# First half's attention: softmax weights moved by a transfer, then transposed as fp32r

## The chip, the cores and the metric

The kernel runs on one core of one Trainium2 chip. The metric is the device time of one execution in microseconds; of the kernel before there are three such runs. One further execution was recorded by the hardware profiler, and everything said of engines, waits and transfers comes from it. The five engines are TensorE (PE; its weight loads are shown apart as PEld), VectorE (DVE), ScalarE (ACT), GpSimd (POOL) and SyncE (SP). SP does no arithmetic here, its queue only issues transfers; POOL's queue issues most of the others.

## The reference, cut to what matters

The program is a two-layer network over 1024 latent tokens and 256 context tokens with 1024 features. Layer 0 mixes tokens with a convolution module, layer 1 with grouped-query attention; each is followed by a SwiGLU feed-forward block. The change lies in the attention of layer 1, for the latent tokens (16 query heads, 4 key/value heads, 64 features a head, 1024 + 256 = 1280 keys):

```python
def gqa_sdpa(q, k, v):
    B, Q, H, Dh = q.shape
    qg = q.reshape(B, Q, N_KV_HEADS, KV_GROUP, Dh)
    s = jnp.einsum("bqkgd,bskd->bkgqs", qg, k).astype(jnp.float32) * (Dh ** -0.5)
    p = jax.nn.softmax(s, axis=-1).astype(v.dtype)
    o = jnp.einsum("bkgqs,bskd->bqkgd", p, v)
    return o.reshape(B, Q, H * Dh)
```

Everything is fp32 in the reference.

## The kernel before, in words

**Arithmetic.** Products of fp32 matrices are made from fp32r operands: a value is split into a high part, rounded to fp32r, and a low part, the rest (`split`, lines 161 and 164; weights in `wload`, lines 144 and 148), and three products are added up (`mm3`, lines 172 to 174).

**The attention's unit.** One unit is one key/value head `t` and 128 queries `qt`: four query heads against 1280 keys. The first half of the queries has 16 units, the second half another 16. A unit has two generators. `scores` (line 1116) multiplies queries and keys for one head at a time into a region of 1280 columns of PSUM; VectorE scales the result into SBUF and finds its minimum (line 1122), ScalarE takes the exponential in place and sums it (line 1124). The place is one of the slots of the list `pring`. `values` goes over ten blocks of 128 keys: four transposes, one for each head, into one bank of PSUM (line 1134, with the constant identity as the moving operand and the softmax weights as the stationary one); a copy to fp32r on ScalarE (line 1137); the low part on VectorE (line 1138); two matmuls with the values' high and low halves, each 512 columns wide (lines 1140 and 1141). At the end the two halves are added and divided by the sums (lines 1145 to 1156), and the result is stored to DRAM (line 1450).

**How they are interleaved.** `attn_stream` goes through the units. After each head's scores of a unit it advances the previous unit's `values` by some blocks, as the tuple `turns` says: 3, 3, 3 and 2 of its eleven steps when at least four slots are free. The program's order is the priority of each instruction; a planner then sets each engine's order before the kernel runs, with its own costs, and takes whatever is ready in its plan with the highest priority. At run time each engine works strictly in that order. `later` (the value matmuls, with `lav` = 40) gives a lower priority.

**The stages around it.** While the first units run, the last three of the four query projections of the right half are pumped in beside them from the background queue `bgq`, at `rate` 0.8. They read the normalised tokens in the tiles T4 and T6 and use T5 for work. When the queue is empty, `attention` takes T5 for three more slots (ten in all), and the score region in PSUM gets a second place (`sring`). After the last unit of the first half, the second half's units start in the background beside the output projection of the first half (`out_proj`), which loads the attention's result into HS, splits it into T6 and T3, and writes T4; the feed-forward block follows. The second half's slots lie in T1 and T5.

**Queues.** In this stage POOL's queue carries the loads of queries (line 1102) and keys (line 1095) and the stores of results (line 1450). SP's queue carries the projection's weights (line 143).

Of the kernel before, what the change touches and what calls it, by code (L numbers as in the profile page):

```python
# [8 lines left out]
F32 = mybir.dt.float32  # L9
F32R = mybir.dt.float32r  # L10
# [5 lines left out]
P = 128  # L16
# [4 lines left out]
TOK = CTX + SEQ  # L21
# [19 lines left out]
NC_, NL = CTX // PH, SEQ // PH  # L41
# [14 lines left out]
class Kern:  # L56
# [51 lines left out]
    def acc(self, n):  # L108
        return self.sp.tile([P, 512], F32, tag="acc", name="acc", bufs=2)[:, :n]

    def tiny(self, shape, name):
        return self.sp.tile(shape, F32, tag=name, name=name, bufs=2)

    @contextmanager
    def later(self, n=32):
# [464 lines left out]
    def shift(self):  # L580

        nc, cv = self.nc, self.cvs["C"]
        self.part = self.tiny([P, NC_], "part")
        nc.vector.tensor_scalar(out=self.part, in0=self.vsum[:, :NC_], scalar1=KT / (KT - 1.0), scalar2=None,
                                op0=ALU.mult)
        self.about = self.by_token(self.part)
        self.cacc = self.acc(CTX)
        for k in range(KT - 1):
            self.centre(k)
            yield  # L590
# [514 lines left out]
    def scores(self, q, rq, kt, slots, Ps, sums):  # L1105

        nc = self.nc
        for h in range(4):
            o = self.sring[self.si % len(self.sring)]
            self.si += 1  # L1110
            sc = self.ps.rearrange("p b n -> p (b n)")[:, o:o + TOK]
            k0 = 0
            while k0 < TOK:
                w = min(512 - (o + k0) % 512, TOK - k0)
                for p in range(2):
                    nc.tensor.matmul(sc[:, k0:k0 + w], lhsT=q[:, h, :], rhs=kt[:, p * TOK + k0:p * TOK + k0 + w],  # L1116
                                     start=p == 0, stop=p == 1)
# [4 lines left out]
            nc.vector.tensor_scalar(out=pt, in0=sc, scalar1=rq[:, h:h + 1], scalar2=None, op0=ALU.mult, op1=ALU.min,  # L1122
                                    accum_out=mn)
            nc.scalar.activation(pt, pt, AF.Exp, bias=mn, scale=-1.0, accum_out=sums[:, 0, h:h + 1])
            Ps.append(pt)
            yield 1.07

    def values(self, t, Ps, sums, dst, done):
        nc, c = self.nc, self.c
        av = self.bank("av")  # L1130
        for j in range(NJ):
            tp = self.bank("pt")
            for h in range(4):
                nc.tensor.transpose(tp[:, h * P:(h + 1) * P], Ps[h][:, j * P:(j + 1) * P], c["ident"])  # L1134
            ph, pl = self.ptring[self.ptslot % len(self.ptring)]
            self.ptslot += 1
            nc.scalar.copy(ph, tp)  # L1137
            nc.vector.tensor_tensor(pl, tp, ph.bitcast(F32), op=ALU.subtract)  # L1138
            with self.later(self.lav):
                nc.tensor.matmul(av, lhsT=self.value(t, j), rhs=ph, start=j == 0, stop=False)  # L1140
                nc.tensor.matmul(av, lhsT=self.value(t, j), rhs=pl, start=False, stop=j == NJ - 1)  # L1141
            yield 0.87
# [16 lines left out]

    def attn_stream(self, units, kts, dst_of, loaded=False):  # L1160

        prev, cur, nq, Ps = None, None, None, []
        for n, (t, qt) in enumerate(units):
            if t != cur:
                if cur is not None and len(kts) == 1 or cur is None and not loaded:
                    self.load_k(t, kts[t % len(kts)])
                cur, kt = t, kts[t % len(kts)]
            q = nq or self.load_q(t, qt)
            nq = self.load_q(*units[n + 1]) if n + 1 < len(units) else None
# [9 lines left out]
            sg = self.scores(q, self.rq[t][:, 4 * qt:4 * qt + 4], kt, slots, Ps, sums)  # L1179
# [250 lines left out]
    def attention(self, final, qr):  # L1430
# [46 lines left out]
        self.sring = [0, TOK]  # L1477
        self.pring = [pr1[:, 0], pr4[:, 0], pr1[:, 1], pr4[:, 1], pr1[:, 2], pr4[:, 2]]
# [245 lines left out]
```

## Time and profile before

| what | value |
|---|---|
| median of 3 runs | 2937.25 us (2936.89 to 2942.66) |
| profiled execution | 2938.98 us |
| its span | 2937.2 us |
| mean granted TensorE clock | 0.987 of full |
| scores of units 5 to 14 of the first half | 1671.3 to 1818.3 us |
| transposes of line 1134 | 1280, from 1588.7 to 2383.6 us |

The time of an execution is a little longer than the span, which goes from its first to its last instruction. Shares of busy time are averages over stages with different limits; the stage in question is some 200 us long, and its own windows are what to read. Durations of neighbouring instructions of an engine overlap, so that the distance from start to start says more of a cost than a duration does.

### The profile page before, as it was taken

How to read it: one execution, taken by the hardware profiler on the slowest of the kernel's cores; microseconds unless marked ns; L12 is line 12 of the kernel's file. 1: busy time of each engine (PE TensorE's matmuls, PEld its weight loads, DVE VectorE, ACT ScalarE, POOL GpSimd, SP SyncE). 2: the span in 40 equal slices, each digit the busy share in tenths (PEclk: the TensorE clock that was granted, in tenths of full speed). 3: DMA queues.
4: the chain of work that ended last, by engine and by line, in shares of the span. 5: the costliest groups of instructions: out<-in, count | busy, mean ns of one | idle time of the engine just before them, and what ended most of it. 6: DMA issues, size and time to landing. Idle time of an engine off the chain costs nothing.

```text
span 2937.2 us, 42731 instructions
## 1 busy us (share of the span) xinstructions
PE 2847.7 (97%) x16462; PEld 2446.1 (83%) x16462; DVE 2160.7 (74%) x3746; ACT 1335.5 (45%) x2229; POOL 222.6 (8%) x377
## 2 busy tenths in 40 slices
PE   7999989999999999999999999989999999999998
PEld 6888877888888889989888787767777778889997
DVE  6887788847556378877786899786666666786777
ACT  5222255532222245544445688645555543444444
POOL 0000001011022001000011111110000000010000
PEclk9999999999999999999999999999999999999999
DMA  6443444334356224333345211322222143353332
GB/s 249 140 120 98 116 131 145 135 116 143 115 175 198 65 74 165 114 104 112 109 156 170 88 46 46 97 87 81 66 73 83 60 149 99 110 170 104 102 98 75
DMA packets 131755, 336.58 MB, mean 115 GB/s; under 512 B 31328, under 2 KB 52864, under 8 KB 130656
## 3 DMA queue, kind: packets, MB, share of 16 engines
q1 hardware_dynamic: 78016, 222.33, 24.1%
q0 software_dynamic: 29344, 103.83, 10.7%
q10 hardware_dynamic: 24192, 7.70, 1.1%
q8 instruction: 129, 2.11, 0.3%
q14 instruction: 74, 0.61, 0.1%
HBM read 289.50 MB, written 38.93 MB: 112 GB/s over the span
## 4 chain that ended last, share of the span: by engine, by line
PE 86%; DVE 7%; ACT 2%; issue 2%; DMA 2%; ACTq 0%; POOL 0%; SPq 0%; DVEq 0%; POOLq 0%
PE ps L172 15%; PE ps L173 15%; PE ps L174 15%; PE ps L875 4%; PE ps L877 4%; PE ps L876 4%; PE ps L1116 4%; PE ps L1134 4%; PE ps L1140 2%; PE ps L454 2%; PE ps L455 2%; PE ps L456 2%; PE ps L1141 2%; PE ps L185 1%; PE ps L183 1%
## 5 line engine op out<-in xcount | busy, mean ns | idle before, releaser
L172 PE MATMUL ps<-T,wh 128*128 128x512 f32 (+1 forms) x1360 | 502.5, 370 | 1.4 <-ACT T L161 0.8
L174 PE MATMUL ps<-T,wl 128*128 128x512 f32 (+1 forms) x1360 | 500.4, 368 | 2.0 <-DVE wl L148 2.0
L173 PE MATMUL ps<-T,wh 128*128 128x512 f32 (+1 forms) x1312 | 481.4, 367 | 0.2 <-DVE T L164 0.2
L144 ACT CAST wh<-wr 128x1024 fp32r<-128x1024 f32 (+1 forms) x217 | 225.0, 1037 | 419.9 <-PE ps L173 307.2
L148 DVE TENSOR_TENSOR wl<-wr,wh 128x1024 fp32r<-128x1024 f32 (+1 forms) x217 | 261.9, 1207 | 168.5 <-ACT wh L144 167.1
L875 PE MATMUL ps<-T,wh 128*128 128x256 f32 x1092 | 310.7, 285 | 5.0 <-ACT wh L161 4.5
L876 PE MATMUL ps<-T,wh 128*128 128x256 f32 x1092 | 306.5, 281 | 0.0
L877 PE MATMUL ps<-T,wl 128*128 128x256 f32 x1092 | 305.4, 281 | 0.2 <-DVE wl L164 0.2
L1138 DVE TENSOR_TENSOR T<-ps,T 128x512 fp32r<-128x512 f32 x320 | 216.8, 687 | 107.6 <-ACT T L1137 106.8
L172 PEld LDWEIGHTS ps<-T,wh 128*128 128x128 f32 x1360 | 257.8, 190 | 43.7 <-ACT T L1506 1.7
L174 PEld LDWEIGHTS ps<-T,wl 128*128 128x128 f32 x1360 | 257.7, 190 | 42.4 <-DVE wl L148 2.2
L173 PEld LDWEIGHTS ps<-T,wh 128*128 128x128 f32 x1312 | 248.5, 189 | 38.2 <-DVE T L164 1.3
L1137 ACT CAST T<-ps 128x512 fp32r<-128x512 f32 x320 | 186.0, 586 | 191.1 <-PE ps L1134 177.6
L173 PE MATMUL ps<-HS,wh 128*128 128x512 f32 x656 | 257.9, 393 | 0.0
L172 PE MATMUL ps<-HS,wh 128*128 128x512 f32 x608 | 238.4, 392 | 0.9 <-ACT wh L144 0.9
L174 PE MATMUL ps<-HS,wl 128*128 128x512 f32 x608 | 237.5, 391 | 0.0
L875 PEld LDWEIGHTS ps<-T,wh 128*128 128x128 f32 x1092 | 206.1, 189 | 11.2 <-ACT wh L161 6.7
L876 PEld LDWEIGHTS ps<-T,wh 128*128 128x128 f32 x1092 | 206.6, 189 | 0.5
L877 PEld LDWEIGHTS ps<-T,wl 128*128 128x128 f32 x1092 | 206.2, 189 | 0.6 <-DVE wl L164 0.4
L1134 PE MATMUL ps<-cst,T 128*128 128x128 f32 x1100 | 189.6, 275 | 3.2 <-DVE T L1138 3.1
L1122 DVE TENSOR_SCALAR_CACHE_REDUCE T<-ps,rq 128x1280 f32<-128x1280 f32 x110 | 170.0, 1546 | 27.9 <-PE ps L1116 22.1
L1134 PEld LDWEIGHTS ps<-cst,T 128*128 128x128 f32 x1100 | 132.6, 141 | 49.5 <-DVE T L1138 30.8
(377 smaller groups left out, 6195.9 us busy)
## 6 DMA issues: line engine op xcount, KB each, us to landing
wr<-in_w SPq DMA_DIRECT2D x170, 512.0 KB, 3.6
wr<-in_pw SPq DMA_DIRECT2D x35, 512.0 KB, 3.5
HV<-in_wmodT POOLq DMA_DIRECT2D x56, 256.0 KB, 4.1
q<-in_wmodT POOLq DMA_DIRECT2D x56, 256.0 KB, 3.9
KB<-in_w SPq DMA_DIRECT2D x24, 512.0 KB, 3.6
HR<-in_w SPq DMA_DIRECT2D x23, 512.0 KB, 3.7
q<-in_w SPq DMA_DIRECT2D x23, 512.0 KB, 4.2
q<-qsd POOLq DMA_DIRECT2D x32, 256.0 KB, 3.3
```

The lines of the kernel that those rows point to most:

```text
L144: nc.scalar.copy(hi, raw)
L148: nc.vector.tensor_tensor(lo, raw, hi.bitcast(F32), op=ALU.subtract)
L172: nc.tensor.matmul(out[:, :n], lhsT=wh, rhs=xh, start=k == 0, stop=False)
L173: nc.tensor.matmul(out[:, :n], lhsT=wh, rhs=xl, start=False, stop=False)
L174: nc.tensor.matmul(out[:, :n], lhsT=wl, rhs=xh, start=False, stop=k == nk - 1)
L875: nc.tensor.matmul(out, lhsT=wh, rhs=bh, start=first and k == 0, stop=False, **skip)
L876: nc.tensor.matmul(out, lhsT=wh, rhs=bl, start=False, stop=False, **skip)
L877: nc.tensor.matmul(out, lhsT=wl, rhs=bh, start=False, stop=k == 3, **skip)
L1122: nc.vector.tensor_scalar(out=pt, in0=sc, scalar1=rq[:, h:h + 1], scalar2=None, op0=ALU.mult, op1=ALU.min, accum_out=mn)
L1134: nc.tensor.transpose(tp[:, h * P:(h + 1) * P], Ps[h][:, j * P:(j + 1) * P], c["ident"])
L1137: nc.scalar.copy(ph, tp)
L1138: nc.vector.tensor_tensor(pl, tp, ph.bitcast(F32), op=ALU.subtract)
```

## The change

It has these parts, all in the attention:

- Once the background queue is empty, T5, T4 and T6 become nine places for copies (`copies`), instead of T5 becoming three more slots. `pring` stays at seven slots.
- For a unit that starts after that, each head's softmax weights, when their exponential is done, are moved by a transfer on SP's queue (640 KB, SBUF to SBUF) from their slot to the next place. Both sides are fp32; the transposes read the copy as fp32r, through a new fp32r identity `idr`, and write PSUM as fp32r. The slots of such a unit are taken in turn.
- From the second such unit on, the previous unit's `values` begin two heads later: no step after the first head's scores, then 2, 3 and 3; their last three steps (two blocks and the closing work) follow the first head's scores of the unit after.
- When the first half's stream has ended, `copies` is emptied and T5 is taken for the second half's slots, whose units run as before.
- `tiny` gets a parameter for its number of buffers, and `part`, of the convolution, has one buffer instead of two.

```diff
@@ shift
-        self.part = self.tiny([P, NC_], "part")
+        self.part = self.tiny([P, NC_], "part", 1)
@@ scores
             nc.scalar.activation(pt, pt, AF.Exp, bias=mn, scale=-1.0, accum_out=sums[:, 0, h:h + 1])
+            if moved:
+                self.ci += 1
+                pc = self.copies[self.ci % len(self.copies)]
+                nc.sync.dma_start(pc, pt)
+                pt = pc
             Ps.append(pt)
@@ values
             for h in range(4):
-                nc.tensor.transpose(tp[:, h * P:(h + 1) * P], Ps[h][:, j * P:(j + 1) * P], c["ident"])
+                pt, to = Ps[h][:, j * P:(j + 1) * P], tp[:, h * P:(h + 1) * P]
+                if moved:
+                    nc.tensor.transpose(to.bitcast(F32R), pt.bitcast(F32R), self.idr)
+                else:
+                    nc.tensor.transpose(to, pt, c["ident"])
@@ attn_stream
+            moved = len(self.copies) > 0
+            if moved and len(free) == len(self.pring):
+                slots = [self.pring[(self.ci + 1 + h) % len(self.pring)] for h in range(4)]
...
+            late = moved and shifted
             for h in range(4):
                 yield next(sg)
-                if prev is not None:
-                    for _ in range(turns[h]):
+                if late and h == 0:
+                    yield from tail or ()
+                elif prev is not None:
+                    for _ in range((0, 2, 3, 3)[h] if late else turns[h]):
                         yield next(prev)
             for _ in sg:
                 pass
-            prev = self.values(t, Ps, sums, *dst_of(t, qt))
+            if late:
+                tail = prev
+            shifted = moved
+            prev = self.values(t, Ps, sums, *dst_of(t, qt), moved)
+        yield from tail or ()
         yield from prev
@@ attention
+        self.idr = self.cp.tile([P, P], F32R, tag="idr", name="idr")
+        nc.scalar.copy(self.idr, c["ident"])
+        self.copies, self.ci = [], 0
...
             elif pr4 is None:
-                pr4 = self.T("T5", [P, 3, TOK])
-                self.pring = self.pring[:4] + [pr4[:, 0], pr4[:, 1], pr4[:, 2]] + self.pring[4:]
+                pr4 = True
+                self.copies = [c[:, i] for c in [self.T(t, [P, 3, TOK]) for t in ("T5", "T4", "T6")] for i in range(3)]
                 self.set_banks(**alone)
                 self.sring = [0, TOK]
         self.lav = 40
 
         self.lo_dve = 1.0
+        self.copies = []
+        pr4 = self.T("T5", [P, 3, TOK])
```

More of the change, by code (lines that the diff above doesn't have):

```diff
@@ L109, in acc, with tiny @@
         return self.sp.tile([P, 512], F32, tag="acc", name="acc", bufs=2)[:, :n]
-    def tiny(self, shape, name):
-        return self.sp.tile(shape, F32, tag=name, name=name, bufs=2)
+    def tiny(self, shape, name, bufs=2):
+        return self.sp.tile(shape, F32, tag=name, name=name, bufs=bufs)
     @contextmanager
@@ L1103, in load_q, with scores @@
         return q.bitcast(F32R)
-    def scores(self, q, rq, kt, slots, Ps, sums):
+    def scores(self, q, rq, kt, slots, Ps, sums, moved=False):
         nc = self.nc
@@ L1124, in scores, with values @@
             nc.scalar.activation(pt, pt, AF.Exp, bias=mn, scale=-1.0, accum_out=sums[:, 0, h:h + 1])
+            if moved:
[3 more added lines that the diff above has]
+                pt = pc
             Ps.append(pt)
             yield 1.07
-    def values(self, t, Ps, sums, dst, done):
+    def values(self, t, Ps, sums, dst, done, moved=False):
         nc, c = self.nc, self.c
@@ L1160, in attn_stream @@
     def attn_stream(self, units, kts, dst_of, loaded=False):
-        prev, cur, nq, Ps = None, None, None, []
+        prev, cur, nq, Ps, tail, shifted = None, None, None, [], None, False
         for n, (t, qt) in enumerate(units):
@@ L1178, in attn_stream @@
             sums = self.sp.tile([P, 2, 4], F32, tag="sums", name="sums", bufs=3)
-            sg = self.scores(q, self.rq[t][:, 4 * qt:4 * qt + 4], kt, slots, Ps, sums)
+            sg = self.scores(q, self.rq[t][:, 4 * qt:4 * qt + 4], kt, slots, Ps, sums, moved)
+            late = moved and shifted
             for h in range(4):
                 yield next(sg)
-                if prev is not None:
-                    for _ in range(turns[h]):
+                if late and h == 0:
+                    yield from tail or ()
+                elif prev is not None:
+                    for _ in range((0, 2, 3, 3)[h] if late else turns[h]):
                         yield next(prev)
```

## The prediction

> **What bounds the kernel now.** I read the page's busy times first, then the TensorE clock, then the one stage the change touches: the first half's attention after the last query projection, about 1657 to 1853 us. There the scores of a unit (one kv head, 128 queries, four heads) repeat with a rhythm of two units, so I cut the stage at the rhythm.
>
> ```profile
> PE 2847.7 (97%) x16462; PEld 2446.1 (83%) x16462; DVE 2160.7 (74%) x3746; ACT 1335.5 (45%) x2229; POOL 222.6 (8%) x377
> ```
>
> ```profile
> core 0: us, PE busy (x) PEld busy (x) DVE busy (x) ACT busy (x) POOL busy (x), PEclk, DMA share, GB/s
> 1671.30:1700.70 29.40, 28.51 (x174) 23.26 (x172) 26.78 (x45) 23.68 (x39) 3.41 (x5) 1.00 0.20 50
> ...
> 1788.90:1818.30 29.40, 28.62 (x175) 23.48 (x173) 26.83 (x46) 23.91 (x41) 4.15 (x7) 1.00 0.31 81
> sum 147.00, PE 143.00 PEld 117.20 DVE 134.14 ACT 119.20 POOL 20.69; mean PE 28.60 PEld 23.44 DVE 26.83 ACT 23.84 POOL 4.14
> ```
>
> Ten units take 147.0 us, 14.70 each, at full clock. Over the whole kernel VectorE is at 74%; here it is at 134.1/147 = 91%, TensorE at 97%. Two engines near their limit: that decides how much a cheaper transpose can bring. The groups and the waits of the same ten units:
>
> ```profile
> L1138 DVE TENSOR_TENSOR T<-ps,T 128x512 fp32r<-128x512 f32 x101 | 67.3, 685 | 10.4 <-ACT T L1137 10.1
> L1137 ACT CAST T<-ps 128x512 fp32r<-128x512 f32 x100 | 57.7, 587 | 25.5 <-PE ps L1134 16.4 <-PE ps L1140 6.2
> ```
>
> ```profile
> ACT T L1137 <- PE ps L1134: 16.4, 26, 1.0
> DVE T L1138 <- ACT T L1137: 10.1, 15, 1.0
> PEld ps L1116 <- DVE T L1122: 4.4, 11, 0.5
> ```
>
> VectorE idles for L1137 on ScalarE, which idles for the transposes (L1134); TensorE waits a little for VectorE to free score banks. TensorE is the first limit, VectorE the next. What each needs per unit comes from distances between starts in the timelines, because durations overlap (here TensorE, then VectorE):
>
> ```profile
> 1762.05 1.03 PE L1134 MATMUL ps<-cst,T 128*128 128x128 f32 x8
> 1762.84 0.48 PE L1141 MATMUL ps<-T,HR 128*128 128x512 f32 x1
> ...
> 1769.50 0.39 PE L1140 MATMUL ps<-T,HR 128*128 128x512 f32 x1
> 1769.73 0.40 PE L1141 MATMUL ps<-T,HR 128*128 128x512 f32 x1
> ```
>
> ```profile
> 1699.45 1.28 DVE L1138 TENSOR_TENSOR T<-ps,T 128x512 fp32r<-128x512 f32 x2
> 1700.65 1.54 DVE L1122 TENSOR_SCALAR_CACHE_REDUCE HS<-ps,rq 128x1280 f32<-128x1280 f32 x1
> 1702.12 0.08 DVE L1122 DVE_READ_ACCUMULATOR HS<-ps,rq 128x1 f32 x1
> ...
> 1718.51 0.41 DVE L1152 TENSOR_TENSOR sb<-ps,sb 64x256 f32<-64x256 f32 x1
> 1718.84 0.67 DVE L1138 TENSOR_TENSOR T<-ps,T 128x512 fp32r<-128x512 f32 x1
> ```
>
> Eight transposes take 0.79 us and lengthen the matmul behind them by 0.08 (0.48 against 0.40): 0.87/8 = 0.109 us each. A 512-column fp32r matmul takes 0.23, a 256-column one about half. Per unit TensorE needs 40 x 0.109 + 36 x 0.233 + 8 x 0.118 + 2 x 0.11 = **13.9 us**. VectorE needs 4 x 1.47 (L1122) + 10 x 0.60 (L1138) + 3 x 0.33 (L1152 and L1156, of like size) + about 0.4 for the reciprocal = **13.3 us**. The rhythm is 14.7, 0.8 above the higher of the two.
>
> **The change part by part.** It acts from the first unit that starts after the background queue is empty. Counting the yields (18.75 us of them at rate 0.8 for three chunks of 5), that falls early in the third unit, so units 4 to 16 are moved: 13 units, 520 transposes, 52 transfers. The second half sets the copies to none and stays as it was.
>
> Transposes in fp32r. No transpose of this type is in the trace; the nearest rows are the short fp32r matmuls of the convolution (L532 324 columns, L533 162) and the weight loads:
>
> ```profile
> 371.85 0.31 PE L532 MATMUL ps<-HS,T 128*128 128x324 f32 x1
> 371.99 0.24 PE L533 MATMUL ps<-HS,T 128*128 128x162 f32 x1
> 372.07 0.34 PE L532 MATMUL ps<-HS,T 128*128 128x324 f32 x1
> ```
>
> ```profile
> L1134 PEld LDWEIGHTS ps<-cst,T x1100: 137/140/231, 1588.5 to 2383.5; 128*128 128x128 f32 x184
> L533 PEld LDWEIGHTS ps<-HS,T x320: 187/190/337, 110.5 to 374.1; 128*128 128x128 f32 x160
> ```
>
> An fp32r matmul of 162 columns hands over after 0.08 us (371.99 to 372.07); scaled to 128 columns, 0.061 us is the low end. But the matmul behind it is then itself longer (0.34 against 0.31), because it waits for its weights: 0.08 + 0.035 = 0.115 to 0.12, the high end, when each short matmul is bound by a load of the 190 ns kind. A transpose's load is of the 140 ns kind, 50 ns shorter, so I take the low end: 0.061. The fourth transpose of a group stays at about 0.115, since the fp32r matmul behind it still needs a long load. A group of four then costs 3 x 0.061 + 0.115 = 0.30 instead of 0.44, ten groups save **1.4 us a unit**, and TensorE's need falls to 12.5.
>
> There is a rule that speaks against this: the Trainium skill, TensorE: Matmul & The Clock Gate, section LDWEIGHTS (loading the stationary operand), puts a load at its columns divided by 1.2, 107 ns for 128, whatever the type. Taken as a floor for each transpose, as today's 0.109 would fit, the new type saves nothing; that is the first rival below. The two kinds of load in this trace, 140 and 190 ns for the same 128 columns, speak against one price for all.
>
> What the unit then takes. VectorE's 13.3 is now the higher need. The ends: 13.3 (no slack lost) and 14.7 (all of it lost to new waits, no gain). Today 0.8 is lost with two engines at 13.9 and 13.3; with the second at 12.5 I take a little less, 0.65: 13.95, **0.75 less per unit**. Of the 13 units I count 12.5, the first one having fewer slots: 12.5 x 0.75 = **9.4 us**.
>
> The transfers. 52 moves of 640 KB (128 x 1280 x 4) go to SP's queue behind the exp of their head. They delay nothing there: between 1640 and 1880 SP issues one transfer.
>
> ```profile
> 1875.10 0.33 SPq L143 DMA_DIRECT2D wr<-in_wo  x1
> ```
>
> ```profile
> wr<-in_w SPq DMA_DIRECT2D x170, 512.0 KB, 3.6
> KB<-ksd POOLq DMA_DIRECT2D x10, 640.0 KB, 7.1
> wr<-in_w SPq DMA_DIRECT2D x12, 384.0 KB, 3.2
> ```
>
> From 384 to 512 KB landing grows by 0.4 us, so 640 KB from SP gives 4.0; the high end is the 7.1 of an equal transfer on POOL's queue, issued in pairs. Four in 13.95 us are 188 GB/s beside the 50 and 81 of the windows above. Is the latency covered? The exps of one unit's last head and of the next unit's first three (ScalarE's timeline; the second and third stand between these):
>
> ```profile
> 1728.97 1.37 ACT L1124 ACTIVATE T<-T,mn 128x1280 f32<-128x1280 f32 x1 [0.16 <-DVE T L1122]
> ...
> 1737.41 1.37 ACT L1124 ACTIVATE HS<-HS,mn 128x1280 f32<-128x1280 f32 x1 [0.32 <-DVE HS L1122]
> ```
>
> The last head's weights are there at 1730.3 and land at 1734.3. The new order puts the first transposes behind two more heads' scores and two left-over transpose groups with their closing work; on VectorE that is 2 x 1.47 + 2 x 0.60 + 1.2 = 5.3 us. So 4.0 is hidden, with 1.3 to spare, and costs nothing; without the cover it is up to 4.0 a unit. Behind a blocked transpose stand, on TensorE's in-order queue, the scores of the third head and the value matmuls, and VectorE starves next.
>
> Slots. The score slots are given back once their move has landed, instead of after the transposes, and seven do where ten were; nine copies in T5, T4 and T6 hold two units. The first moved unit finds three free slots, its fourth head waits for unit 3's transposes: 0 to 2 us, I take 1. The one fp32r identity copy and the single buffer for `part`, used once, cost nothing.
>
> The end of the stage. T6 now holds weights until the last transpose of unit 16, and the output projection splits into T6. Today the splits start beside the last transposes and the projection follows:
>
> ```profile
> 1852.81 1.14 ACT L161 CAST T<-HS 128x512 fp32r<-128x512 f32 x2
> ...
> 1859.85 0.60 PE L1134 MATMUL ps<-cst,T 128*128 128x128 f32 x4
> ...
> 1864.30 0.39 PE L172 MATMUL ps<-T,wh 128*128 128x512 f32 x1
> ```
>
> So some 7 us of lead (1852.8 to 1859.9) are lost to the splits. In return pr1's slots are free at once for the second half's first scores, which fill TensorE and VectorE meanwhile. Ends: -2 and +5; I take +0.5. **Sum:** -9.4 + 1 + 0.5 = -7.9. The profiled execution took 2938.98 us around its span of 2937.2, and becomes 2931.1; it stands 1.7 above the shown median of 2937.25, so the median becomes **2929.3**. What follows the stage keeps its work and shifts.
>
> **The rivals.** First, the transpose gets no cheaper: 0.115 to 0.12 instead of 0.109, 520 x 0.01 = +5 us at most on TensorE, partly inside today's 0.8 of slack, plus 1.5 at the edges. For it: the longer matmul behind L533; against it: the shorter load. About 2940. Second, the wait for the move takes the place of the wait for the transposes, which ends slower: it decides from a latency of 5.3 us on. At the 7.1 of the ksd row each unit waits 1.8 and loses it on top of 13.95, 15.75 a unit: 12.5 x 1.05 = +13, with the edges 2952. For it: 640 KB rows at 7.1; against it: SP's large loads all land in 3.2 to 3.7, and the order is planned with other scores to run first. Third, VectorE, ScalarE and two transpose banks keep their hand-over losses: 14.3 a unit instead of 13.95, 12.5 x 0.4 = -5, with the edges -3.5: 2934. For it: L1138 waits for L1137 and not only for TensorE; against it: 16.4 of L1137's 25.5 us of waiting are for transposes.
>
> **How the numbers follow.** A measurement of this kernel can tell about 0.2%, 5.9 us, from no change. Forecast 0.52, first rival 0.20, second 0.16, third 0.12. The forecast's own range is 2922 (13.4 a unit) to 2935. It is faster by more than 5.9 in about four fifths, 0.42, else the same; the first rival is the same in 0.13 and slower in 0.06; the second slower in 0.13, the same in 0.03; the third the same in 0.10, faster in 0.02. Together with 0.01 faster for a first rival that still frees slots: faster 0.45, same 0.36, slower 0.19. For 8 in 10 the range goes from 2921 to 2946.
>
> **What would show it.** Right: L1134 starts about 0.06 apart, VectorE at 95% or more in the stage, its waits for L1137 shrunk, the scores of ten units in some 140 us. Wrong: L1134 still 0.11 apart with loads of 190 ns (first rival); TensorE idle before L1134 released by a transfer, and moves landing after more than 5 us (second); VectorE below 94% with unmoved waits for ScalarE (third); or a gap before the first projection matmul of more than the 5 us allowed.

## The result and the profile after

The changed kernel takes 2954.54 us (median of 4 runs, 2951.66 to 2958.33), the kernel before 2938.74 us beside it (4 runs): ratio 1.0053, 95% interval 1.0035 to 1.0070. It is slower, where 2929.3 was forecast and 2946 was the upper end of the range.

The profiled execution took 2951.66 us, its span is 2949.9. Line numbers have moved: 1122 is still the eviction of scores (scaling and minimum) and 1124 the exponential, 1128 is the new move, 1141 the fp32r transpose, 1146 ScalarE's copy, 1147 VectorE's low part, 1149 and 1150 the value matmuls, 1161 and 1165 the closing work. The page's busy times and its rows on the moves (count, KB, median us from issue to landing):

```profile
PE 2846.4 (96%) x16462; PEld 2443.5 (83%) x16462; DVE 2162.3 (73%) x3746; ACT 1337.1 (45%) x2230; POOL 221.6 (8%) x377
...
T<-HS SPq DMA_DIRECT2D x31, 640.0 KB, 5.5
...
T<-T SPq DMA_DIRECT2D x21, 640.0 KB, 5.9
```

The 52 moves are the ones counted. TensorE's busy time hardly fell, and it has idle time that it did not have. The last instruction of each unit (the multiplication by the reciprocal, one a unit) shows where. First before, then after, nine of them, from unit 5 to unit 13 (first and last start):

```profile
L1156 DVE TENSOR_TENSOR sb<-sb,ps x9: 409/410/410, 1709.1 to 1826.7; 128x256 f32<-128x256 f32 x9
```

```profile
L1165 DVE TENSOR_TENSOR sb<-sb,ps x9: 410/410/420, 1714.4 to 1843.5; 128x256 f32<-128x256 f32 x9
```

Eight units took 117.6 us, 14.70 each, and now take 129.1, 16.14 each. From the last unit's closing (1868.8 before, 1885.2 after) to the end of the span are 1068.4 and 1064.7 us. So the stage lost 16.4 us at its end, what follows it gained 3.7, and the sum is the 12.7 us between the two spans.

So 5.3 us were lost before unit 5 closed, 11.5 in these eight units, and 0.4 came back in the last three.

Were the transposes cheaper? TensorE's timeline of after (start, duration; x4 is one group of four transposes, and the square brackets say how long TensorE stood idle before and for what):

```profile
1678.35 0.49 PE L1141 MATMUL ps<-idr,T 128*128 128x128 f32 x2 [2.72 <-DMA T<-HS]
...
1749.96 0.46 PE L1141 MATMUL ps<-idr,T 128*128 128x128 f32 x4
1750.26 0.47 PE L1149 MATMUL ps<-T,HR 128*128 128x512 f32 x1
...
1773.15 0.87 PE L1141 MATMUL ps<-idr,T 128*128 128x128 f32 x8
1778.96 1.22 PE L1116 MATMUL ps<-T,q 128*128 128x256 f32 x3 [4.94 <-DVE T L1122]
```

Yes, by half of what was forecast. A group of four takes 0.30 us to the start of the next matmul (1749.96 to 1750.26). But that matmul is then longer itself, and the prediction's 0.44 for the kernel before had such a lengthening in it. Pieces of the chain of waits (the profile's path back from the last instruction, at each step to what released it) give a group and the matmul behind it by one measure, before first, then after:

```profile
1741.41 0.44 PE ps L1134 x4
1741.85 0.23 PE ps L1141
```

```profile
1750.12 0.30 PE ps L1141 x4
1750.42 0.30 PE ps L1149
```

That is 0.67 us before and 0.60 now. A group became 0.07 cheaper, some 0.7 us a unit: half of the 1.4 that was forecast, and TensorE's need falls from 13.9 to some 13.2, not to 12.5.

The other rows of the timeline are two long waits of TensorE in the stage. Ahead of 1678.35, in the first moved unit, it waits 2.72 us for a move, directly. Between 1773 and 1779 it waits 4.94 us for VectorE's eviction, and VectorE in turn waits for moves that still read the slot into which it has to write:

```profile
1777.34 1.55 DVE L1122 TENSOR_SCALAR_CACHE_REDUCE T<-ps,rq 128x1280 f32<-128x1280 f32 x1 [3.60 <-DMA T<-T]
...
1784.27 1.55 DVE L1122 TENSOR_SCALAR_CACHE_REDUCE HS<-ps,rq 128x1280 f32<-128x1280 f32 x1 [2.61 <-DMA T<-HS]
```

SP's queue in that stretch, and behind it the row of the second half's first key load on POOL's queue (both are of 640 KB a transfer):

```profile
1769.07 0.47 SPq L1128 DMA_DIRECT2D T<-T  x1
...
1771.90 1.52 SPq L1128 DMA_DIRECT2D T<-HS  x1
```

```profile
L1095 POOL DMA_DIRECT2D KB<-ksd x2: 540/542/545, 1769.2 to 1770.5; - x2
```

Four moves were issued within 2.8 us, because the places for them became free together, and two key loads stood between them. The view of line 1128, for 1640 to 1700 us and then for 1700 to 1900, gives the landing (least, median, most):

```profile
DMA to landing us min/median/max: 3.2/3.5/7.0
...
DMA to landing us min/median/max: 3.2/6.2/15.5
```

What the waits cost by windows (length, then busy time of each engine, the granted clock of TensorE, share of the transfers, GB/s):

```profile
1670.42:1695.89 25.47, 21.73 (x124) 17.36 (x122) 21.34 (x35) 19.66 (x32) 2.67 (x4) 0.93 0.72 242
...
1768.00:1777.30 9.30, 6.02 (x42) 5.01 (x40) 4.72 (x10) 5.98 (x12) 2.24 (x4) 1.00 0.82 206
1777.30:1795.70 18.40, 16.25 (x86) 12.94 (x86) 13.59 (x22) 11.26 (x19) 1.94 (x3) 0.81 0.70 219
```

The direct wait is 2.72 us, the idle time of TensorE in the last two rows 3.28 + 2.15 us. The clock, at 1.00 in the same stretch before, takes up to 0.07 x 25.47 = 1.8 and 0.19 x 18.40 = 3.5 us more. That is an estimate of 13.4 us at most: a part of TensorE's ordinary idle time is in it, and for 2.61 us of the slow stretch VectorE waited for a move anyway.

### The profile page after: what moved, and what is told of

Read it like the earlier page. It is cut to its first block, busy times and chain, and to the rows that moved or that the text cites. A ratio compares the mean times of both kernels' runs of the same rounds, so it can differ in the third digit from the quotient of the medians.

```text
span 2949.9 us, 42874 instructions
## 1 busy us (share of the span) xinstructions
PE 2846.4 (96%) x16462; PEld 2443.5 (83%) x16462; DVE 2162.3 (73%) x3746; ACT 1337.1 (45%) x2230; POOL 221.6 (8%) x377
## 3 DMA queue, kind: packets, MB, share of 16 engines
q0 software_dynamic: 29344, 103.83, 10.8%
## 5 line engine op out<-in xcount | busy, mean ns | idle before, releaser
L1122 DVE TENSOR_SCALAR_CACHE_REDUCE T<-ps,rq 128x1280 f32<-128x1280 f32 x91 | 140.8, 1547 | 31.0 <-PE ps L1116 21.5
L926 DVE TENSOR_TENSOR T<-ps,T 128x512 f32<-128x512 f32 (+1 forms) x168 | 110.1, 661 | 67.9 <-PE ps L174 66.1
L1116 PE MATMUL ps<-KB,q 128*128 128x512 f32 (+1 forms) x576 | 140.8, 367 | 8.2 <-DVE T L1122 4.6
```

## Experiments on the change: one part taken out at a time

Four kernels, each the changed one less one part. In the expectations M is the theory that the moves cost the time (landing, waits for a place), O that the later order of the values does, G that cheaper transposes are worth what the prediction gave them, S that the planned order of engines that work strictly in order does not turn shorter transposes into time.

**e1: no moves.** The exponential writes its result into the place for copies itself, rounded to fp32r.

```diff
-            nc.scalar.activation(pt, pt, AF.Exp, ...)
+            pc = pt
 ...
-                nc.sync.dma_start(pc, pt)
-                pt = pc
+            nc.scalar.activation(pc, pt, AF.Exp, ...)
+            pt = pc
 ...
-                self.copies = [... self.T(t, [P, 3, TOK]) ...]
+                self.copies = [... self.T(t, [P, 3, TOK], F32R) ...]
```

> The moves are left out: in a moved unit the exponential writes the next of the nine places itself, as fp32r; slots, places, order and fp32r transposes stay as in the changed kernel. This leaves out the low part of the first half's softmax weights (they are rounded to fp32r), so the subtraction on VectorE has nothing left to find, but it is still done. Theory M (the loss is the transfer: its landing, and its wait for a place that the transposes of two units before give back, put late behind VectorE's and TensorE's in-order queues): without it the units finish some 13.6 to 14.4 us apart and the time is 2925 to 2938. Theory O (the order is the loss: values two heads later, scores run ahead until nine places are full): ScalarE then waits for places instead of SP, the units stay at 15 us or more and the time is 2945 to 2960.

2956.29 us, 1.0059 (1.0042 to 1.0075).

**e2: fp32 transposes from the moved copies.**

```diff
-                    nc.tensor.transpose(to.bitcast(F32R), pt.bitcast(F32R), self.idr)
+                    nc.tensor.transpose(to, pt, c["ident"])
```

> The changed kernel with transposes in fp32 from the copies; everything else as changed. Both theories: the loss is not in the transposes, whose gain is now missing: M and O expect 2955 to 2972. If the fp32r transposes brought nothing because VectorE was the limit all the time, it stays at the changed kernel's 2951 to 2958.

2956.42 us, 1.0059 (1.0044 to 1.0074).

**e3: twelve places** (T1 too) and four slots. The first moved unit's scores overwrite slots that the third unit's values have still to read, so that a part of this unit's result is not the attention's.

```diff
-            if moved and len(free) == len(self.pring):
+            if moved:
 ...
-                self.copies = [... for t in ("T5", "T4", "T6")] for i in range(3)]
+                self.copies = [... for t in ("T5", "T4", "T6", "T1")] for i in range(3)]
+                self.pring = [prh[:, i] for i in range(4)]
```

> Twelve places (T1 too) and four slots instead of nine and seven. M: a move then waits for the transposes of three units before, which are long done, so moves are issued right after their exponential instead of in bursts; the gap at 1768 to 1797 us goes; 2932 to 2945. If the landing time alone is the loss, or the order (O): 2948 to 2960.

2956.1 us, 1.0054 (1.0039 to 1.0069).

**e4: the order of before**, with all the rest of the change.

```diff
-            late = moved and shifted
+            late = False
```

> The changed kernel with the values' order of before (3, 3, 3 and 2 steps after the heads of the next unit, no tail). M: the moves' landing is then hidden less, places come back a little earlier: within 6 us of the changed kernel's 2954, on either side. O: most of the 16 us come back, 2938 to 2945.

2956.65 us, 1.0054 (1.0039 to 1.0069).

None of the four gives anything back. Theory M missed e1 and e3, theory O missed e4, and e2 lies in every range that was given for it. Read one by one, that would acquit every part, though together they cost 15.8 us. The chain of waits of e1 (three units of it, 1780.8 to 1828.6, summed by line) shows why such runs don't add up:

```profile
by line: ACT T L1128 17.0%; ACT T L1146 13.5%; DVE T L1147 12.5%; PE ps L1149 10.7%; PE ps L1116 10.7%; PE ps L1150 9.6%; PE ps L1141 7.6%; DVE HS L1122 6.2%; issue 5.5%; DVE T L1122 3.1%; ACT sb L1160 2.3%; PE ps L1164 1.4%; ACTq L1146 0.1
```

Without the moves the chain goes through ScalarE's exponentials (L1128 there) and copies; TensorE's lines are 40% of it. The planner orders every engine anew for each kernel, and e1 loses its time in another place than the changed kernel, about as much. So the next runs started from the other side: the kernel before, and one part added.

## Experiments from the kernel before: no moves at all

**f1: fp32r transposes alone.** Slots and order of before; the slots are fp32r, so scores and exponentials are written there rounded; units 4 to 16 are transposed as fp32r.

```diff
-        pr1 = self.T("T1", [P, 3, TOK])
-        prh = self.T("HS", [P, 4, TOK])
+        pr1 = self.T("T1", [P, 3, TOK], F32R)
+        prh = self.T("HS", [P, 4, TOK], F32R)
 ...
+                if moved:
+                    nc.tensor.transpose(to.bitcast(F32R), pt, self.idr)
```

> The kernel before with its ten slots and its order; the only change of time is that units 4 to 16 transpose as fp32r. So that they may, the slots are fp32r tiles that the scaled scores and the exponential are written into, rounded (in both halves): this changes the computation by that rounding, and adds no instruction but the identity's copy. Theory G (a cheaper transpose alone is worth what the prediction said, and the rest of the change eats it): 2925 to 2933. Theory S (the planned order of the engines does not gain from a shorter transpose, or gets worse with it: TensorE then waits for score banks that VectorE gives back in its own fixed order): 2936 to 2950.

**f2: the same with sixteen slots and the later order.**

```diff
+                self.pring = self.pring + [x[:, i] for x in [pr4] + [self.T(t, ...) for t in ("T4", "T6")] for i in range(3)]
 ...
+                    slots = [self.pring[(self.si16 + h) % 16] for h in range(4)]
 ...
-            late = fr and shifted and False
+            late = fr and shifted and True
```

> As the one before, but with sixteen slots in turn (T5, T4, T6 beside the seven) and the changed kernel's order (values two heads later); no moves. G: close to it, 2925 to 2936. If the later values cost by themselves (theory O): 2945 to 2960, like the changed kernel.

**f3: as f2, with fp32 slots and transposes.**

```diff
-                    nc.tensor.transpose(to.bitcast(F32R), pt, self.idr)
+                    nc.tensor.transpose(to, pt, c["ident"])
```

> The kernel before with sixteen slots in turn and values two heads later, fp32 transposes, no moves, nothing rounded. O: 2945 to 2962. If the order is harmless: 2935 to 2942.

**f4: as f3, with the order of before**, so that sixteen slots taken in turn (and the one buffer for `part`) are all that differs from before.

```diff
-            late = fr and shifted and True
+            late = fr and shifted and False
```

> The kernel before with sixteen slots in turn and its own order; fp32 transposes, no moves, nothing rounded. It tells what holding T4 and T6 to the end of the stage and a turn of sixteen slots cost: both theories 2936 to 2943; if T6's late return to the output projection is the loss, 2944 or more.

| kernel | us | ratio to before (2940.12) |
|---|---|---|
| f1: fp32r | 2945.75 | 1.0016 (1.0006 to 1.0025) |
| f2: fp32r, 16 slots, later | 2944.86 | 1.0013 (1.0004 to 1.0023) |
| f3: 16 slots, later | 2949.6 | 1.0030 (1.0021 to 1.0040) |
| f4: 16 slots | 2942.9 | 1.0005 (0.9996 to 1.0015) |

More slots do nothing (f4). The later order alone costs 2949.6 - 2942.9 = 6.7 us; with cheap transposes it costs nothing in sum (f2 against f1). And the cheap transposes alone, the very thing the change is for, come with 0.16% more time instead of 0.3% less: theory G falls. f1's closings of units 5 to 13:

```profile
L1160 DVE TENSOR_TENSOR sb<-sb,ps x9: 408/409/414, 1708.7 to 1827.9; 128x256 f32<-128x256 f32 x9
```

14.90 us a unit instead of 14.70, 1.6 us over the eight. The last unit closes at 1874.1 us instead of 1868.8, so that most of f1's loss falls later, in units 14 to 16. There TensorE waited 0.29, 0.58 and 1.35 us in short succession (1852.8 to 1856.0), and the granted clock fell. Before first, then f1:

```profile
1857.00:1875.00 18.00, 16.46 (x86) 13.08 (x85) 15.79 (x26) 12.38 (x20) 4.34 (x6) 1.00 0.48 154
```

```profile
1857.00:1875.00 18.00, 17.40 (x79) 13.24 (x78) 15.21 (x25) 11.67 (x20) 5.08 (x7) 0.85 0.37 121
```

0.15 x 18 = 2.7 us is an estimate of what the clock takes there. In the steady units the question is why nothing was gained. TensorE's waits between 1671.3 and 1818.3 us (us in total, times, longest), before and then f1:

```profile
PE ps L1116 <- DVE HS L1122: 2.9, 5, 0.7
PE ps L1116 <- DVE T L1122: 1.1, 5, 0.2
```

```profile
PE ps L1116 <- DVE T L1122: 5.4, 9, 0.9
PE ps L1116 <- DVE HS L1122: 5.4, 9, 0.9
```

These are all the waits of TensorE there: 4.0 us, 0.40 a unit, before, and 10.8 us, 1.09 a unit, in f1. So 0.7 us a unit more, as much as the cheaper transposes give, goes into waiting for VectorE's eviction of scores (L1122). TensorE's busy time itself fell by only 0.5 a unit (143.00 and 136.19 of the 147 us), and the rest is the 0.2 by which the unit grew. TensorE comes to the next score region sooner and finds VectorE still emptying it. The chain of waits over these eight units, summed by line, takes the same turn; first before, then f1 (L1136 is f1's transpose, L1144 and L1145 its value matmuls, L1142 its low part, L1141 its copy):

```profile
by line: PE ps L1134 22.2%; PE ps L1116 19.5%; PE ps L1140 15.2%; PE ps L1141 14.3%; DVE T L1138 8.2%; issue 7.9%; ACT T L1137 4.1%; DVE HS L1122 2.5%; DVE T L1122 2.2%; DVE sb L1152 2.2%; PE ps L1155 1.5%; ACT sb L1151 0.4%
```

```profile
by line: PE ps L1116 20.2%; PE ps L1145 14.1%; PE ps L1136 13.9%; PE ps L1144 13.3%; DVE T L1142 8.1%; DVE HS L1122 7.9%; DVE T L1122 7.9%; issue 6.6%; ACT T L1141 3.5%; DVE sb L1156 2.7%; PE ps L1159 1.5%; ACT T L1124 0.4%; ACTq L1124 0.0%
```

TensorE's lines fall from 72.7% to 63.0%, and the eviction goes from 4.7% to 15.8%. These shares show the path and not the price: once TensorE waits for an eviction at all, however briefly, the chain runs through the whole of it. Two such places in one unit of f1, in TensorE's timeline, have waits of 0.19 and 0.94 us:

```profile
1746.65 0.97 PE L1116 MATMUL ps<-KB,q 128*128 128x256 f32 x4 [0.19 <-DVE T L1122]
...
1752.41 0.73 PE L1116 MATMUL ps<-KB,q 128*128 128x256 f32 x3 [0.94 <-DVE T L1122]
```

## Is it one hand-over, or one engine?

**The bank of the value sums (g1 to g4).** There is one PSUM bank for the sums, and its closing work (two copies, two additions, two transposes, a product) queues among other work. A steady unit of f1, TensorE's timeline: the unit's first value matmul, its last, and the next unit's first.

```profile
1739.02 0.47 PE L1144 MATMUL ps<-T,HV 128*128 128x512 f32 x1
...
1748.60 0.47 PE L1145 MATMUL ps<-T,HR 128*128 128x512 f32 x1
...
1753.97 0.46 PE L1144 MATMUL ps<-T,HV 128*128 128x512 f32 x1
```

The value matmuls take 9.6 us, and then the bank is closed to the next unit for 5.4. Theory V made this the limit. The edit lets the second copy follow the first, with a place of its own, and plans the closing work ahead; g1 has it in the kernel before, g2 in f1, g3 in the changed kernel. g4 takes the bank out with one copy in f1 and adds on POOL.

```diff
-        tmp = self.sb(256).rearrange("p (a q) -> p a q", q=P)
+        t2 = self.sb(256)
+        tmps = [x.rearrange("p (a q) -> p a q", q=P) for x in (rt[:, 256:512] if fast else t2, t2)]
 ...
+        with self.later(-100 if fast else 0):
+            for b, r, o in ((0, slice(0, 64), slice(64, 128)), (1, slice(64, 128), slice(0, 64))):
+                nc.scalar.copy(tmps[b][r], v[o, :, b, :])
```

> The kernel before with one edit in its closing work (units 3 or 4 to 16 of the first half): the two copies of the value sums go to two places instead of one, so that the second need not wait for the first addition, and the closing work gets an earlier place in the plan. Two theories are told apart. Theory V: a unit's length is its stretch of value matmuls plus the time for which the one PSUM bank of the value sums is closed to the next unit (from the last value matmul of a unit to the first of the next: 5.4 us in every steady unit of before, of the changed kernel and of the in-place versions); a shorter hand-over of 3.5 to 4 us shortens the unit, in this kernel only until TensorE's 13.9 us a unit: 14.0 to 14.2 instead of 14.7, so 2930 to 2935. Theory S (no one place; the plan as a whole): the hand-over gets shorter and the stretch longer by the same, 2936 to 2942.

> The same edit in the version with softmax weights rounded in place, fp32r transposes, before's slots and order, and no moves (2945.75, units of 14.9). Theory V: with transposes of 0.06 us TensorE leaves room, so the whole shortening of the hand-over shows: units of 13.2 to 13.8, 2926 to 2933, and faster than the same edit with fp32 transposes. Theory S: 2942 to 2948.

> The same edit in the changed kernel (moves, later order, 2954.5, units of 15.7 between closings). Theory V: 10.1 of value stretch plus 3.5 to 4, so units of 13.6 to 14.3, 2935 to 2944, the stall at the second half's key load (some 5 us) staying. Theory S: 2950 to 2957.

The edit of g4:

```diff
+                nc.scalar.copy(avs, av)
 ...
+                    nc.gpsimd.tensor_copy(tmp[r], v[o, :, b, :])
+                    nc.gpsimd.tensor_tensor(dst[r], v[r, :, b, :], tmp[r], op=ALU.add)
```

> The in-place fp32r version again, with the bank of the value sums taken out by one 128x512 copy on ScalarE (some 0.6 us), then GpSimd's copies and additions from SBUF and one multiplication on VectorE. Theory V: a hand-over near 3 us, units of 13 to 13.6, 2923 to 2931; VectorE loses 0.8 us of additions a unit. Theory S: 2940 to 2948, or slower, if GpSimd's work closes later than the next unit needs it.

Beside before's 2941.09: g1 2947.3 us, 1.0023 (1.0012 to 1.0033); g2 2944.28, 1.0012 (1.0002 to 1.0021); g3 2959.36, 1.0065 (1.0050 to 1.0080); g4 2958.43, 1.0060 (1.0044 to 1.0077). The same three matmuls of g2, and then its closings:

```profile
1738.65 0.47 PE L1145 MATMUL ps<-T,HV 128*128 128x512 f32 x1
...
1749.56 0.46 PE L1146 MATMUL ps<-T,HR 128*128 128x512 f32 x1
...
1753.35 0.47 PE L1145 MATMUL ps<-T,HV 128*128 128x512 f32 x1
```

```profile
L1165 DVE TENSOR_TENSOR sb<-sb,ps x9: 408/409/411, 1708.9 to 1826.0; 128x256 f32<-128x256 f32 x9
```

The hand-over fell to 3.8 us, as meant, and the stretch of value matmuls grew from 9.6 to 10.9: 14.64 a unit in g2 against 14.90, where V said 13.2 to 13.8. Theory V falls. S is not confirmed by that throughout: g1 and g3 came out slower than either theory said. In g4 VectorE's product (L1163) waits for POOL's additions; its row for 1690 to 1830 us (us in total, times, longest):

```profile
DVE sb L1163 <- POOL sb L1162: 16.3, 8, 2.1
```

**Each engine made lighter (h1 to h4, i1, i2).** All start from f1. h1 leaves out VectorE's subtraction and keeps TensorE's work, so that the value sums of its units 4 to 16 come out doubled; h2 leaves out the second value matmul and keeps the subtraction; h3 leaves out both; h4 plans the eviction of scores ahead; i1 leaves out every second copy on ScalarE; i2 is h3 with every second copy on VectorE. In f1 the weights are rounded before they are transposed, so h2, h3 and i2 lose nothing more by leaving out the low part; in i1 the subtraction takes off again what the first product adds, so the sum stays the weights, other than its expectation says. Theory C is the round through ScalarE and VectorE, T a fixed loss beside TensorE's work, A ScalarE as the limit. The expectations take TensorE's need in f1 as 12.5 us a unit; with the transposes as measured it is some 13.2.

```diff
h1:
-            nc.vector.tensor_tensor(pl, tp, ph.bitcast(F32), op=ALU.subtract)
+            if moved:
+                pl = ph
h2, h3:
-                nc.tensor.matmul(av, lhsT=self.value(t, j), rhs=pl, ...)
+                if not moved:
+                    nc.tensor.matmul(av, lhsT=self.value(t, j), rhs=pl, ...)
h4:
+            with self.later(-200 if self.fr else 0):
+                nc.vector.tensor_scalar(out=pt, in0=sc, ...)
i1:
-            nc.scalar.copy(ph, tp)
+            if not moved or j % 2 == 0:
+                nc.scalar.copy(ph, tp)
i2:
+            if moved and j % 2:
+                nc.vector.tensor_copy(ph, tp)
```

> The in-place fp32r version (weights rounded in place, before's slots and order, no moves; 2945.75, units of 14.9) without the subtractions of VectorE in the moved units; the second value matmul reads the high part again, so TensorE's work stays and the value sums of these units come out doubled. Theory C (TensorE waits for a round through ScalarE and VectorE: copy, subtraction, eviction of scores): VectorE falls from 13.3 to 7.3 us a unit, the round no longer binds, units of 12.6 to 13.2, near TensorE's 12.5: 2917 to 2925. Theory T (a fixed loss of some 2.3 us a unit beside TensorE's work): 14.6 to 14.9 as before, 2942 to 2948.

> The same version with the subtractions kept and the second value matmul left out in the moved units (the weights are rounded to fp32r before they are transposed, so the low part adds nothing): TensorE loses 10 x 0.233 = 2.3 us a unit, VectorE nothing. Theory C: the round through VectorE stays, units of 14.0 to 14.8, 2936 to 2946. Theory T: 2.3 less, 12.5, 2913 to 2919.

> The same version without either, subtraction or second value matmul. TensorE needs 10.2 us a unit, VectorE 7.3, ScalarE 12.0 (119.7 in 147 us of ten units). Theory C: ScalarE is next, units of 12.3 to 12.8: 2912 to 2920. Theory T: 10.2 + 2.3 = 12.5, about the same; this run says how far the stage can go, not which theory is right.

> The in-place version with all its work, and only the eviction of scores (scaling and minimum, VectorE) planned ahead of subtractions and closing work. Theory C: the scores' banks come free sooner, TensorE waits less, units of 14.0 to 14.5, 2933 to 2942. Theory T: 14.6 to 14.9, 2942 to 2948.

> The in-place fp32r version (2945.75, units of 14.9) without ScalarE's copy of the transposed weights in every second block of the moved units; the subtraction and the first value matmul there read what an earlier unit left in that place, so the result of these units is not the attention's. ScalarE falls from 12.3 to some 9.4 us a unit; TensorE's 12.5 and VectorE's 13.3 stay. Theory A (ScalarE is what the unit waits for): 13.4 to 13.9, near VectorE's need: 2925 to 2934. Theory S (no single engine; the fixed orders pass a saving on as waiting): 14.5 to 15.1, 2941 to 2950.

> The version without subtraction and second value matmul (2929.91, units of 13.7), with every second copy of the transposed weights done by VectorE instead of ScalarE: TensorE 10.2, VectorE some 10.3, ScalarE 9.4 us a unit. Theory A: units of 11 to 12.5, 2895 to 2915. Theory S: 13 to 14, 2921 to 2934.

The closings of units 5 to 13 of h1, h2, h3, i1 and i2, one fence each:

```profile
L1163 DVE TENSOR_TENSOR sb<-sb,ps x9: 416/420/422, 1714.0 to 1832.1; 128x256 f32<-128x256 f32 x9
```

```profile
L1161 DVE TENSOR_TENSOR sb<-sb,ps x9: 408/408/421, 1708.7 to 1830.0; 128x256 f32<-128x256 f32 x9
```

```profile
L1162 DVE TENSOR_TENSOR sb<-sb,ps x9: 415/416/419, 1712.5 to 1822.0; 128x256 f32<-128x256 f32 x9
```

```profile
L1161 DVE TENSOR_TENSOR sb<-sb,ps x9: 408/409/411, 1712.3 to 1828.7; 128x256 f32<-128x256 f32 x9
```

```profile
L1165 DVE TENSOR_TENSOR sb<-sb,ps x9: 420/420/423, 1705.5 to 1805.9; 128x256 f32<-128x256 f32 x9
```

The shares below are busy times in the window 1709 to 1827 us over its 118 us; the rows of f1, h1 and i2 as examples:

```profile
sum 118.00, PE 109.07 PEld 86.53 DVE 106.64 ACT 94.98 POOL 16.71; mean PE 109.07 PEld 86.53 DVE 106.64 ACT 94.98 POOL 16.71
```

```profile
sum 118.00, PE 112.33 PEld 87.88 DVE 59.99 ACT 94.72 POOL 17.27; mean PE 112.33 PEld 87.88 DVE 59.99 ACT 94.72 POOL 17.27
```

```profile
sum 118.00, PE 110.54 PEld 86.28 DVE 97.90 ACT 85.39 POOL 21.55; mean PE 110.54 PEld 86.28 DVE 97.90 ACT 85.39 POOL 21.55
```

| kernel | unit, us | PE, DVE, ACT busy | us | ratio |
|---|---|---|---|---|
| before | 14.70 | 97, 91, 81% | | |
| f1 | 14.90 | 92, 90, 80% | 2945.75 | 1.0016 (1.0006 to 1.0025) |
| h1, DVE lighter | 14.76 | 95, 51, 80% | 2939.31 | 0.9995 (0.9985 to 1.0004) |
| h2, PE lighter | 15.16 | 86, 89, 79% | 2948.68 | 1.0024 (1.0014 to 1.0034) |
| i1, ACT lighter | 14.55 | 93, 93, 65% | 2940.73 | 1.0008 (0.9998 to 1.0017) |
| h3, PE and DVE lighter | 13.69 | 87, 54, 85% | 2929.91 | 0.9962 (0.9947 to 0.9977) |
| i2, all three shared out | 12.55 | 94, 83, 72% | 2914.22 | 0.9915 (0.9900 to 0.9929) |

Lighten one engine, whichever, and the unit stays between 14.55 and 15.16 us, with the lightened engine idle: VectorE at 51% in h1, ScalarE at 65% in i1. Each of the theories C, T and A named one place, and each is missed by a unit: C by h1, T by h2, A by i1. With both low parts gone the unit falls to 13.69, and with ScalarE's copies shared out as well to 12.55. h4 (2965.92 us, 1.0083, 1.0068 to 1.0098) shows the other side: the same work, one operation planned earlier, and the last unit closes 22.3 us later than in f1 (1896.4 against 1874.1).

Theory S fits h1, h2 and i1 (i1's 2940.73 us lies just under its 2941): three engines in fixed orders, with two places each for scores and for transposed weights between them, pass a saving on one on as waiting on the next.

But S is not shown. i2 came out at 2914.22 us, in the range of theory A (2895 to 2915) and faster than S said (2921 to 2934). And a plainer reading fits the table as well: in every row one engine is busy for 87 to 97% of the unit, TensorE in h1 (95%), i1 (93%, and VectorE the same) and i2 (94%), VectorE in h2 (89%). By that reading the busiest engine sets the unit, with 0.4 us of idle time before and 0.7 to 1.8 us in the versions from f1 on, and lightening one of three nearly equal engines could not give much. No run separates the two readings. What the runs do show is that the loss beside the busiest engine did not stay what it was before.

i2 beats both kernels, by some 25 us against before (2939.1 beside it) and by more against the changed one. It computes the softmax weights less finely: rounded to fp32r, without a low part in units 4 to 16.

## Why the prediction was wrong

**"What the unit then takes" is the step that failed.** It took the need of the busiest engine and added a loss: 13.3 + 0.65 = 13.95, 0.75 less a unit. Measured without moves (f1): 14.90, 0.2 more. The loss over the higher need went from 0.8 to 1.6 us, while the need fell only by 0.6, from 13.9 to 13.3. The quoted row "PEld ps L1116 <- DVE T L1122: 4.4" was read as a small wait; it was the place where TensorE's saved time ended up, with waits of TensorE that went from 0.40 to 1.09 us a unit. The sign that the prediction named for being right, VectorE at 95% or more, did not come: 90% in f1, and 86% in the changed kernel (101.83 of 118 us from 1709 to 1827). The third rival, hand-over losses that stay, had the mechanism but gave it 14.3; h1, i1 and g2 show that shortening one hand-over or one engine does not take such a loss away.

**The transposes** were forecast too cheap. They start 0.06 us apart at first, as taken, and the first rival, a transpose no cheaper, fell. But the sum let the last one of a group pay 0.115 for the matmul behind it and came to 0.30 a group; with that matmul's lengthening a group costs 0.37, 0.07 less than before instead of 0.14. That alone would not have turned the forecast, since the sum went by VectorE's 13.3; it puts TensorE's 13.2 right beside it, where the sum had a gap of 0.8. The Trainium skill, TensorE: Matmul & The Clock Gate, section LDWEIGHTS (loading the stationary operand), puts a load at its columns divided by 1.2, 107 ns for 128, which the prediction considered as the least for each transpose; the trace, with four in 0.37 us, 0.09 each, says otherwise for this type.

**"The transfers ... cost nothing"** failed too. Landing was 3.5 us for the first thirteen, near the 4.0 of the sum, and 6.2 in the median, up to 15.5, for the later 39. The sum took one move at a time, with a cover of 5.3 us before the first transposes. From 1721 us on the moves of the trace go off four at a time, since a place becomes free only when the unit two earlier is done, and two key loads came between. With twelve places (e3) they go off singly until 1766 us, which bears this out; but e3's units took 15.8 us there all the same (1718.5 to 1765.9, at a granted clock of 0.95), so the bursts are not the whole loss. The second rival (a wait for the move in place of the wait for the transposes, 2952) had the sign, and came within 3 us of the measured time by luck: its wait was in the wrong place, not in front of each unit's transposes, but once there (2.72 us) and then at the slots, where VectorE waited 3.60 and 2.61 us for moves that still read them, and f1's loss is not in it. The sentence on nine copies that "hold two units" costed this at nothing.

What the moves add is best read against f2, which has the same order and transposes without moves. The closings of four units without a long wait, f2 first, then the changed kernel:

```profile
L1160 DVE TENSOR_TENSOR sb<-sb,ps x4: 409/410/412, 1710.6 to 1757.8; 128x256 f32<-128x256 f32 x4
```

```profile
L1165 DVE TENSOR_TENSOR sb<-sb,ps x4: 410/410/411, 1714.4 to 1761.6; 128x256 f32<-128x256 f32 x4
```

Both take 47.2 us for three units, 15.73 each, a good 1 us above before: there the moves cost nothing, and the unit is longer all the same. The next two units, with the waits at the slots, take 31.6 us in f2 (to 1789.4) and 37.0 in the changed kernel (to 1798.6).

**Slots, end of the stage.** The +1 for slots has no run of its own: f4 adds slots to the kernel before and finds nothing, and in the trace of the changed kernel VectorE waits for no slot in the first moved unit; its loss is the wait for its move. The end was put at +0.5, between -2 and +5; by one execution of each kernel it gave back 3.7 us, outside these bounds, though executions of the kernel before lie up to 5.8 us apart.

**What stays open.** The waits that can be seen in the changed kernel's trace, 13.4 us at most, are about what lies between its last closing and those of f1 and f2 (1885.2 against 1874.1 and 1871.8). But f2 also rounds its weights in place and has other slots, and no run shows the moves' share by itself: a version without them is planned otherwise (e1). A run of the changed kernel without the second half's early key load was not made. And why the loss beside the busiest engine doubled, by the fixed orders or by engines that are now nearly equal, is not shown.

## What to carry to other kernels

Where three engines stand at 80 to 97% in one stage and hand each other two buffers, don't price a saving as "need of the next engine plus the loss of today": ask of the waits who empties the buffer that the faster engine will reach sooner, and expect little until all the engines of the round get lighter. When a short matmul gets cheaper, count the matmul behind it as well, before and after by the same measure. A transfer put between two engines needs its latency in the burst in which its buffers come free, beside whatever other transfers fall there, and not its median alone. When single parts are taken out of a kernel whose order is planned anew each time, equal times don't acquit the parts; look at the chain of each.

## What the hardware showed

An fp32r transpose of 128x128, four in a row between other matmuls, costs TensorE about 0.09 us with the lengthening of the matmul behind (0.37 a group) against 0.11 in fp32 (0.44). Moves of 640 KB within SBUF landed in 3.2 us at best and 15.5 at worst in one stage, with the same queue and size. And a wait of TensorE costs more than its length: around and behind the wait of 4.94 us, which ended at 1778.96, the granted clock was 0.81 between 1777.3 and 1795.7 us. The Trainium skill, TensorE: Matmul & The Clock Gate, section Why this matters for your kernels, warns of gaps over some 3 us; here the window with the 2.72 us wait has 0.93, and f1 has 0.85 from 1857 to 1875 us behind three waits of which the longest was 1.35, so less was enough.
